# A hybrid attention and recurrence layer on one core: 24 more Strassen pairs in place of 48 classical projection blocks, with the recurrence before the attention

## The chip, the core and the metric

The kernel runs on one core of one Trainium2 chip. The metric is the device time of one execution in microseconds (us). Five engines work side by side, each with its own instruction stream taken in order: TensorE (PE in the profile; its weight loads are PEld), VectorE (DVE), ScalarE (ACT), GpSimd (POOL) and SyncE (SP). They meet at semaphores. Transfers are issued from the streams of SP, ACT and POOL.

## The reference

One layer on 528 tokens (16 learned meta tokens and 512 of x; the reference pads to 640 and drops the padding and the meta tokens at the end), width 2048:

```python
h = rms_norm(x, norm_g)
proj = h @ w_in                       # 2048 x 12368
(q_a, k_a, v_a, z_a, q_i, k_i, w_i, q_b, f_b, i_b, z_b, gates) = jnp.split(proj, cuts, axis=-1)
...
o_a = dsa_attention(q, k, v, qi, ki, wi, chunk_ids, topk)   # 8 heads, top 128 keys of an indexer
y_a = o_a.reshape(B, T, BRANCH_WIDTH) * jax.nn.silu(z_a)
...
o_b = hgrn2_chunkwise(qb, 1.0 - f, vb, jnp.log(f))          # 8 heads of a gated recurrence
y_b = rms_norm(o_b, hgrn_out_norm_g).reshape(...) * jax.nn.silu(z_b)
p = jnp.einsum('btnc,ncd->btnd', y, w_branch)               # two products, 1024 x 2048 each
g = jax.nn.sigmoid(gates)
return x + jnp.sum(g * p, axis=2) @ w_out                   # 2048 x 2048
```

All is float32. Keys, values, forget gates (f_b) and recurrence inputs (i_b) are needed at the meta tokens too; queries, z and gates are not.

## The kernel before

Tokens lie along the columns. hH and hL hold the normalised input, transposed, as 16 tiles of 128 x 528: a high part, and what the high part leaves of the float32 value. Each weight chunk is split in the same way (line 374: ScalarE copies the high part wh, VectorE subtracts for the low part wl), and a product is three matmuls: high by high, high by low, low by high (line 1440).

**Classical blocks.** A job "in" (lines 1413 to 1423) makes 128 columns of the projection out of 16 such tiles of 128 rows: 48 matmuls of 512 columns, or, where the meta tokens are needed, 96 of 264 columns in two PSUM banks. The order is indexer keys, indexer queries, z of attention, keys, values, queries, then by head q, f and i of the recurrence, and z of the recurrence last.

**Strassen pairs.** The gates are made two blocks at a time (run_pair, line 1153). The products of a 2 x 2 split of weights and tokens are done with seven multiplications of half size in place of eight: 7 x 8 x 3 = 168 matmuls of 256 columns, over weight sums s1 to s4 and token sums t1 to t4. The token sums are made once (tops_task, line 1112), the weight sums for each pair: s1 and s2 by VectorE into tiles of their own (lines 401 to 410), s3 and s4 by accumulating DMA from GpSimd's queue (line 112). VectorE combines the products into the two gate blocks, ScalarE applies the sigmoid, SP writes them to DRAM (d_pair, line 1382). The output product uses eight pairs of the same kind (run_out, line 1234).

**What sets the order.** The program is written out by hand with a planner in it. Core (line 43) counts a clock for each engine from fixed costs, while instructions are emitted; attention, recurrence and indexer are generators (tasks) that yield the time at which they can go on, and pump (line 219), called between matmuls of a block, runs a task's next step when its time has passed on the TensorE clock by 300 ns (MARGIN) and VectorE's clock isn't too far ahead. finish (line 231) drives a task to its end with nothing between. Buffers come from 67 slots of 128 x 528 and six PSUM banks of 512 columns and a double one. Weight chunks of 512 KB are loaded from SP's queue into a ring of six, and split two or three products ahead (split_upto, line 364).

Attention runs beside the query blocks, the recurrence beside its own blocks, and a recurrence head waits until all attention heads are through (line 896). Before the first gate pair all tasks are finished (line 1514). y of both branches goes through DRAM (spill_y, line 749); load_y (line 1319) brings it back for the branch products, whose 16 steps load two gate blocks each (req_br, line 1395). After the branch products, m_task (line 1333) makes the token sums for the output.

Of the kernel before, what the change touches and what calls it, by code (L numbers as in the profile page):

```python
# [16 lines left out]
D = 2048  # L17
# [22 lines left out]
MARGIN = 300.0  # L40


class Core:
# [68 lines left out]
    def dma_add(self, out, a):  # L112
        self.nc.gpsimd.dma_start(out, a, accum_op=OP.add)
        return self.at("pool", 4000.0, [out], [out, a])
# [64 lines left out]
def hybrid_kernel(ctx, tc, x, meta, vecs, w_in, rows, w_branch, w_out,  # L179
# [8 lines left out]
    S = Slots(E, sp, [f"s{i}" for i in range(67)], [128, T], None)  # L188
# [42 lines left out]
    def finish(t):  # L231
        while not t.done:
            pump(1e9)
            if t.done:
                break
            nxt = [u for u in tasks if u.t > E.clk["pe"]]
            if nxt:
                E.clk["pe"] = max(E.clk["pe"], min(u.t for u in nxt))
            else:
                assert any(u.step() for u in list(tasks)), "stuck"  # L240
# [8 lines left out]
    def pair(name, keep=0):  # L249
        while len(B2.free) <= keep:  # L250
            yield WAIT
        return B2.get(name)

# [54 lines left out]

    w_in2 = w_in[0]
# [17 lines left out]
    class Pair:  # L327

        def __init__(self, kind, c0, c1, k0, k1, nk, ncols, n=0, done=None, more=()):
            self.kind, self.c0, self.n, self.done, self.nk, self.ncols = kind, c0, n, done, nk, ncols
            self.meta, self.pre, self.req, self.more = False, None, None, more
            self.raw = {}
            for nm, c, k in (("11", c0, k0), ("21", c1, k0), ("22", c1, k1), ("12", c0, k1)):
                ch = self.raw[nm] = {"job": self, "k0": k, "nk": nk, "c0": c, "ncols": ncols, "i": len(stream)}
                stream.append(ch)
            self.ops = []
            for nm in ("11", "s2", "12", "s3", "s1", "22", "s4"):
# [4 lines left out]
    state = {"dma": 0, "split": 0}  # L344
    early = []
    NRAW = 6
    NWS = 3
# [26 lines left out]
    def hi_lo(k, src, m):  # L374
# [3 lines left out]
        (E.ptt if k < 6 else E.tt)(l[:, :m], src, h[:, :m].bitcast(F32), OP.subtract)  # L378
# [22 lines left out]
    def sum_1(pr):  # L401
        if not hasattr(pr, "s1"):
            load_upto(pr.raw["22"]["i"])
            pr.s1 = wp.tile([128, 1024], F32, name=f"sum1_{pr.raw['11']['i']}", tag="s1")
            E.tt(pr.s1, pr.raw["21"]["raw"], pr.raw["22"]["raw"], OP.add)

    def sum_2(pr):
        if not hasattr(pr, "s2"):
            pr.s2 = wp.tile([128, 1024], F32, name=f"sum2_{pr.raw['11']['i']}", tag="s2")
            E.tt(pr.s2, pr.s1, pr.raw["11"]["raw"], OP.add)  # L410

    def sum_3(pr):
        if not hasattr(pr, "s3"):
            pr.s3 = pr.raw["21"]["raw"]
            E.dma_add(pr.s3, pr.raw["11"]["raw"])

    def sum_4(pr):
        if not hasattr(pr, "s4"):
            pr.s4 = pr.raw["12"]["raw"]
            E.dma_add(pr.s4, pr.s2)  # L420

    def prep_op(k, op):

        pr, nm = op["pair"], op["name"]
        first = pr.raw["11"]["i"]
        load_upto(first + (0 if nm == "11" else 2 if nm == "s2" else 3))
        raw = {c: ch["raw"] for c, ch in pr.raw.items() if "raw" in ch}
        if nm in raw:
            src = raw[nm]
        else:  # L430
            for f in (sum_1, sum_2, sum_3, sum_4)[:int(nm[1]) if nm != "s1" else 1]:
                f(pr)
            src = {"s1": pr.s1, "s2": pr.s2, "s3": raw["21"], "s4": raw["12"]}[nm]
        h, l = hi_lo(k, src, 1024)
# [3 lines left out]
        used = {"s3": 2, "22": 3, "s4": 4}.get(nm)  # L438
        if used:
            load_upto(first + used - 1 + NRAW)  # L440

# [154 lines left out]
    def idx_task(j, xq):  # L596
# [18 lines left out]
        if not score:  # L615
            score.extend(slots("score", 4))
# [30 lines left out]
        if not idx_left[0]:  # L647
            S.put(kkH, kkL, CQ, SQ)
            for qt in range(4):
                topk_tasks.append(spawn(topk_task(qt), 6))  # L650

    topk_tasks = []
    bias = [cp.tile([128, k], BF16, name=f"bias{k}") for k in KQ]

    def topk_task(qt):
        kq = KQ[qt]
        sc = score[qt][:, :kq]
        E.dve([sc], [], 64, lambda v: v.memset(sc[0:64, kq - 64:kq], NEG))
        ws = slot("tk")
        w = ws[:, :kq]  # L660
        m8 = cp.tile([128, 8], F32, name=f"m8_{qt}")
        src = sc
        for r in range(TOPK // 8):
            E.dve([m8], [src], kq, lambda v: v.max(m8, src))
            e = E.dve([w], [src, m8], kq, lambda v: v.match_replace(w, m8, src, NEG))
            src = w
            yield e
        E.tt(w, w, sc, OP.is_equal)
        e = E.ts(bias[qt], w, BIAS, None, OP.mult)
        S.put(ws, score[qt])  # L670
        yield e


    kTH, kTL, vH, vL = {}, {}, {}, {}
    vx3 = []
    kx = {}
# [10 lines left out]

    def ka_task(g, xk):
        kx[g] = xk
# [9 lines left out]
        yield e  # L699
        kTH[g], kTL[g] = slot("kTH", F32R), slot("kTL", F32R)  # L700
# [3 lines left out]
        if len(kTH) == 4:  # L704
            pb = yield from bank("pkm")
            for i in range(4):
                e = E.tr(pb[:16, 128 * i:128 * i + 128], kx[i][:, 0:16], ident)
            S.put(*kx.values())
            yield e
            y, e = yield from norm_rope(pb[:16].rearrange("p (b d) -> p b d", b=4), 16, 4,  # L710
                                        tabK[:16, 4:5, :].to_broadcast([16, 4, 64]), "km")
            B1.put(pb)
            yield e
            pb = yield from bank("pkm")
            e = back_T(y, 16, pb)
            yield e
            for i in range(4):
                e = split_T(kTH[i], pb[:, 16 * i:16 * i + 16], 1, kTL[i], 0, 16)
            S.put(y)
            B1.put(pb)  # L720

    def va_task(g, xv):
        pb = yield from bank("pva")
# [3 lines left out]
        vH[g], vL[g] = slot("vH", F32R), slot("vL", F32R)  # L727
        if not vx3:
            vx3.extend((slot("vMH", F32R), slot("vML", F32R), slot("v3")))
        vMH, vML, v3 = vx3  # L730
        E.act(vH[g][:, :512], pb, AF.Copy)
        e = E.tt(vL[g][:, :512], pb, vH[g][:, :512].bitcast(F32), OP.subtract)
        e = E.act(v3[:, 128 * g:128 * g + 128], pb[:, 384:512], AF.Copy)
# [6 lines left out]
        gs = slice(128 * g, 128 * g + 128)  # L740
        E.act(vMH[:16, gs], pm[:16, :128], AF.Copy)
        e = E.tt(vML[:16, gs], pm[:16, :128], vMH[:16, gs].bitcast(F32), OP.subtract)
# [3 lines left out]
    zs = {}  # L746
    yd = [[tc.dram_tile([128, 512], F32, name=f"yd{n}_{h}") for h in range(8)] for n in range(2)]

    def spill_y(n, h, s, e):
        yield e  # L750
        nc.sync.dma_start(yd[n][h], s[:, :512])
        S.put(s)

# [3 lines left out]
    def qa_task(h, xq, prev):  # L757
        g = h // 2
        pb = yield from bank("pqa")
# [9 lines left out]
        yield e  # L769
        qH, qL = slot("qH", F32R), slot("qL", F32R)  # L770
# [4 lines left out]
        while prev and not prev.done:  # L775
            yield WAIT
        for t in topk_tasks + ka_tasks + va_tasks:
            while not t.done:
                yield WAIT
        sm = small[h % 2]  # L780
        ps, pbs, vs = {}, {}, {}
        for qt in (3, 2, 1, 0):
            kq = KQ[qt]
            sl = slice(128 * qt, 128 * qt + 128)
            if kq > 512:
                pb = yield from pair("plg")
                parts = [(pb[:, c, :264], slice(264 * c, 264 * c + 264)) for c in range(2)]
                vs[qt] = pb[:, :, :264]
            else:
                pb = yield from bank("plg")  # L790
                parts = [(pb[:, :kq], slice(0, kq))]
                vs[qt] = pb[:, :kq]
            pbs[qt] = pb
# [4 lines left out]
            if qt == 3:  # L798
                e3 = e
        S.put(qH, qL)  # L800
        yield e3
        col = lambda qt, i: sm[:, 4 * qt + i:4 * qt + i + 1]
        for qt in (3, 2, 1, 0):
            kq = KQ[qt]
            xs = ps[qt] = slot("lg")
            f2 = (lambda a: a.rearrange("p (a b) -> p a b", a=2)) if kq > 512 else (lambda a: a)
            E.dve([xs, sm], [pbs[qt], bias[qt]], kq, lambda vv: vv.tensor_tensor_reduce(
                f2(xs[:, :kq]), vs[qt], f2(bias[qt][:, :]), SC, NEG, OP.add, OP.max, col(qt, 0)))
            (B2 if kq > 512 else B1).put(pbs[qt])
            E.ts(col(qt, 1), col(qt, 0), -1.0, None, OP.mult)  # L810
            e = E.act(xs[:, :kq], xs[:, :kq], AF.Exp, bias=col(qt, 1), accum_out=col(qt, 2))
            if qt == 3:
                e3 = e
        yield e3
        for qt in (3, 2, 1, 0):
            E.dve([sm], [sm], 1, lambda vv: vv.reciprocal(col(qt, 3), col(qt, 2)))
            e = E.ts(ps[qt][:, :KQ[qt]], ps[qt][:, :KQ[qt]], col(qt, 3), None, OP.mult)
        pv_tasks.append(spawn(pv_task(h, ps, e), 1))
# [3 lines left out]
    def pv_task(h, ps, e):  # L822
        g = h // 2
        gs = slice(128 * g, 128 * g + 128)
# [4 lines left out]
        vMH, vML, v3 = vx3  # L829
        po = yield from bank("pov")  # L830

        def turn(b):
# [6 lines left out]
            if b >= 0 and b < 3:  # L839
                S.put(ps[b])  # L840
            if b == 2:
                S.put(ps[3])
# [4 lines left out]
        for b in (3, -1, 0, 1, 2):  # L847
            n = 512 - 128 * max(b, 0)
            kp = 128 if b >= 0 else 16
            if b == 3:  # L850
                tH, tL = slot("pT"), None
                e = E.act(tH[:, :n], pb[:, :n], AF.Copy)
            else:
# [771 lines left out]
```

## Time and profile before

| | |
|---|---|
| median of 3 runs | 1593.71 us (1593.67 to 1596.26) |
| span of the profiled execution | 1593.3 us |
| busy: TensorE, VectorE, ScalarE, GpSimd | 1577.0, 1008.1, 587.4, 112.2 us |
| DMA | 200.94 MB, mean 126 GB/s |
| granted TensorE clock | 0.999 |

Stages by the timeline: start and indexer to about 160 us, z of attention to 241, attention's blocks to 482, recurrence blocks to 830, z of the recurrence to 932, gate pairs to 1250, branch products to 1430, output to the end.

How to read it: a row of a group has line, engine, operation, tile written and tiles read, shapes, count, then busy us in all and mean ns of one, then idle time before and what ended it. A row of a timeline has start, length, engine, line, operation and tiles. A row of windows has the stretch, its length, busy time and count for each engine, granted clock, DMA share and GB/s. A row of transfers has tiles, queue, count, size and median us from issue to landing. Matmuls overlap in the pipeline, so that the lengths of two add up to more than the time between their starts.

### The profile page before, as it was taken

To read this page: it belongs to the slowest core of one execution; us is meant where nothing else is said; L and a number is where in the kernel's file an instruction comes from. 1 tells how busy PE (TensorE), PEld (TensorE's weight loads), DVE (VectorE), ACT (ScalarE), POOL (GpSimd) and SP (SyncE) were. 2 spreads that over 40 slices of the span, in tenths; PEclk is the share of its full clock that TensorE was granted. 3 is DMA by queue.
4 is the path that set the end of the run, shared out by engine and by line. 5 is a ranking of instruction groups with operands and counts; after the bars stand their busy time and mean duration, and the time that the engine had idled before them with its cause. 6 is when DMAs were issued, how large, how long until landed. Compare 5 with 4: busy or idle time off the path is not lost.

```text
span 1593.3 us, 28292 instructions
## 1 busy us (share of the span) xinstructions
PE 1577.0 (99%) x11752; PEld 1427.3 (90%) x11752; DVE 1008.1 (63%) x1773; ACT 587.4 (37%) x910; POOL 112.2 (7%) x108
## 2 busy tenths in 40 slices
PE   7999999999999999999999999999999999999998
PEld 6888889998889888889997899999999888889998
DVE  6687899436666545444444886666666543778765
ACT  5555422324444222222222344444444331334342
POOL 3100000000000000000000000000000000002222
PEclk9999999999999999999999999999999999999999
DMA  9222333232232232222232457777777864448783
GB/s 255 80 68 79 99 93 93 81 91 75 60 79 74 74 81 67 80 68 79 68 81 80 120 128 186 186 186 186 186 187 184 255 198 132 145 120 225 212 215 90
DMA packets 284817, 200.94 MB, mean 126 GB/s; under 512 B 9428, under 2 KB 263904, under 8 KB 284688
## 3 DMA queue, kind: packets, MB, share of 16 engines
q1 hardware_dynamic: 272208, 167.58, 36.9%
q0 software_dynamic: 6976, 25.25, 9.1%
q10 hardware_dynamic: 5504, 6.29, 1.2%
q8 instruction: 92, 1.51, 0.4%
q14 instruction: 37, 0.30, 0.1%
HBM read 157.16 MB, written 16.78 MB: 109 GB/s over the span
## 4 chain that ended last, share of the span: by engine, by line
PE 97%; DVE 1%; DMA 1%; issue 1%; ACT 1%; POOL 0%; DVEq 0%; ACTq 0%; POOLq 0%
PE pg L90 57%; PE po L88 10%; PE py L88 6%; PE px L88 6%; PE pz L88 5%; PE pw L88 3%; PE phl L90 1%; PE pov L88 1%; PE psc L90 1%; PE plg L90 1%; PE pho L90 1%; PE ppt L94 1%; PE phs L90 1%; PE px L94 1%; PE pqa L94 0%
## 5 line engine op out<-in xcount | busy, mean ns | idle before, releaser
L104 DVE TENSOR_TENSOR wl<-raw,wh 128x1024 fp32r<-128x1024 f32 x276 | 339.9, 1232 | 241.3 <-ACT wh L98 237.4
L90 PE MATMUL pg<-hH,wh 128*128 128x264 f32 (+1 forms) x1392 | 478.8, 344 | 0.0
L98 ACT ACTIVATE wh<-raw 128x1024 fp32r<-128x1024 f32 x278 | 294.2, 1058 | 491.4 <-PE pg L90 258.9
L90 PE MATMUL pg<-hH,wl 128*128 128x264 f32 (+1 forms) x1392 | 464.1, 333 | 0.0
L90 PE MATMUL pg<-hL,wh 128*128 128x264 f32 (+1 forms) x1392 | 462.6, 332 | 0.0
L90 PEld LDWEIGHTS pg<-hH,wl 128*128 128x128 f32 x1392 | 261.6, 188 | 26.3
L90 PEld LDWEIGHTS pg<-hL,wh 128*128 128x128 f32 x1392 | 262.3, 188 | 21.1
L90 PEld LDWEIGHTS pg<-hH,wh 128*128 128x128 f32 x1392 | 261.7, 188 | 21.7
L88 PE MATMUL po<-wh,mh 128*128 128x256 f32 x896 | 159.4, 281 | 0.5 <-DVE xq L104 0.5
L88 PEld LDWEIGHTS po<-wh,mh 128*128 128x128 f32 x896 | 137.7, 189 | 0.8 <-DVE xq L104 0.7
L88 PE MATMUL po<-wl,mh 128*128 128x256 f32 x448 | 125.9, 281 | 0.0
L90 PE MATMUL pg<-yH,wh 128*128 128x512 f32 x256 | 101.1, 395 | 0.4 <-ACT yH L98 0.4
L90 PE MATMUL pg<-yL,wh 128*128 128x512 f32 x256 | 100.9, 394 | 0.3 <-DVE yL L104 0.3
L90 PE MATMUL pg<-yH,wl 128*128 128x512 f32 x256 | 100.9, 394 | 0.0
L88 PEld LDWEIGHTS po<-wl,mh 128*128 128x128 f32 x448 | 84.3, 188 | 0.0
L104 DVE TENSOR_TENSOR wl<-sum,wh 128x1024 fp32r<-128x1024 f32 x48 | 64.9, 1352 | 29.7 <-ACT wh L98 29.7
L98 ACT ACTIVATE wh<-sum 128x1024 fp32r<-128x1024 f32 x48 | 50.9, 1061 | 84.0 <-PE pw L88 27.5
L88 PE MATMUL px<-hL,wh 128*128 128x256 f32 x256 | 72.5, 283 | 0.0
L88 PE MATMUL px<-hH,wl 128*128 128x256 f32 x256 | 72.0, 281 | 0.0
L88 PE MATMUL px<-hH,wh 128*128 128x256 f32 x256 | 71.6, 280 | 0.0
L90 PEld LDWEIGHTS pg<-yL,wh 128*128 128x128 f32 x256 | 48.2, 188 | 12.3 <-DVE yL L104 1.1
L90 PEld LDWEIGHTS pg<-yH,wh 128*128 128x128 f32 x256 | 48.0, 187 | 11.9 <-ACT yH L98 0.8
(309 smaller groups left out, 2594.7 us busy)
## 6 DMA issues: line engine op xcount, KB each, us to landing
raw<-in_w_in_dram SPq DMA_DIRECT2D x192, 512.0 KB, 3.9
raw<-in_w_branch_dram SPq DMA_DIRECT2D x32, 512.0 KB, 4.5
raw<-in_w_out_dram SPq DMA_DIRECT2D x32, 512.0 KB, 4.2
raw<-raw POOLq DMA_DIRECT2D x24, 512.0 KB, 5.4
raw<-sum POOLq DMA_DIRECT2D x24, 512.0 KB, 6.3
gd<-gate SPq DMA_DIRECT2D x32, 256.0 KB, 5.9
g<-gd SPq DMA_DIRECT2D x30, 256.0 KB, 3.0
x<-in_x_dram SPq DMA_DIRECT2D x16, 256.0 KB, 5.4
```

Of the source, the lines that this page charges most:

```text
L88: self.nc.tensor.matmul(out, lhsT, rhs, start=start, stop=stop, skip_group_check=True)
L90: self.nc.tensor.matmul(out, lhsT, rhs, start=start, stop=stop)
L94: self.nc.tensor.transpose(out, in_, ident)
L98: self.nc.scalar.activation(out, in_, f, **kw)
L104: self.nc.vector.tensor_tensor(out, a, b, op=op)
```

## The change

Of the classical blocks only the indexer's and z of attention stay. The other 48 are coupled into 24 pairs of the same kind as the gate pairs: f with q and i with z of each recurrence head, keys with two query heads and values with the other two, each time one block that needs the meta tokens with one that doesn't. The 11 and 12 products, which go to the x bank, take the meta columns along (272 columns). The order becomes recurrence pairs, attention pairs, gate pairs; attention's tasks start once the eighth recurrence head is done, group by group. The branch products begin with the recurrence's branch (ORDER), and y of attention is due at their step 4. A block that waits for its task goes to DRAM when fewer than eight slots are free (hold), and is fetched back on ScalarE's queue (held). The weight sums are made in the loaded chunks themselves, in another order of the seven products; of each split, VectorE's half is put off until the third k step of the next product. That frees room for four more slots. Gates are written without sigmoid, which ScalarE does in the branch stage. Token sums are made beside the z blocks. The meta keys' three matmuls with values become one over 96 rows. One task does top-k for the four query blocks in turn, and some steps of the softmax and the recurrence go from VectorE to ScalarE.

```diff
+NZA = 8
+NSLOT = 71
+ORDER = (1, 0)
+LIMIT = 2000.0
+ROOMY = 8
...
+    SEVEN = (("11", "11", "x", 0), ("s3", "t3", "y", 0), ("12", "21", "x", 1), ("s2", "t2", "v", 0),
+             ("s1", "t1", "z", 0), ("22", "t4", "w", 0), ("s4", "22", "z", 1))
...
+    def sum_w(pr, nm):
+
+        if nm in pr.did:
+            return
+        pr.did.add(nm)
+        load_upto(pr.first + {"s3": 1, "s2": 2, "s1": 2, "s4": 3}[nm])
+        r = {c: ch["raw"] for c, ch in pr.raw.items() if "raw" in ch}
+        if nm == "s3":
+            E.dma_add(r["21"], r["11"])
+        elif nm == "s2":
+            E.tt(r["21"], r["21"], r["22"], OP.add)
+        elif nm == "s1":
+            E.tt(r["11"], r["21"], r["11"], OP.subtract)
+        else:
+            E.dma_add(r["12"], r["21"])
...
     def ka_task(g, xk):
-        kx[g] = xk
+        while not (len(pv_tasks) >= 2 * g and pv_tasks[2 * g - 1].done if g else len(hg_tasks) == 8 and hg_tasks[7].done):
+            yield WAIT
+        xk = yield from held("xk", xk)
+        yield from room(2)
...
+    def fetch(name, of, q, n=512):
+        s = slot(name)
+        q.dma_start(s[:, :n], of[:, :n])
+        E.wr[s.tensor.name] = (E.clk["pe"] + 4000.0, "dma")
+        return s
+
+    def hold(s, n=T):
+
+        if len(S.free) >= ROOMY:
+            return s, None, None, n
+        state["held"] += 1
+        d = tc.dram_tile([128, n], F32, name=f"held{state['held']}")
+        return None, d, spawn(spill(d, s, E.wr[s.tensor.name][0], n), 0), n
+
+    def held(name, x):
+        s, d, t, n = x
+        if s is None:
+            while not t.done:
+                yield WAIT
+            yield from room(1)
+            s = fetch(name, d, nc.scalar, n)
+            yield E.wr[s.tensor.name][0]
+        return s
...
+            elif b < 0:
+                E.mm(o, vm[0:96, 0:128], tH[0:96, :n], False, False, loose=True)
                 S.put(tH)
...
             for k in range(8):
-                th, tl = TB[k][tn]
+                th, tl = TB[k][tn + "m" if wide else tn]
                 st_ = k == 0 and not on_
                 E.mm(b, op["h"][k], th, st_, False, loose=True)
                 E.mm(b, op["h"][k], tl, False, False, loose=True)
                 E.mm(b, op["l"][k], th, False, k == 7, loose=True)
+                if k == WHEN:
+                    flush()
+                    if i == 0:
+                        sum_w(pr, "s2")
+                        sum_w(pr, "s1")
+                pump(LIMIT)
...
             if last:
-                if i == 3:
-                    S.put(*hH[:8], *hL[:8])
-                    ysplit = split_y(load_y(0), 0)
-                elif i == 4:
-                    S.put(*[t for k in range(8) for t in TB[k]["tiles"][:2]])
+                if i == 4:
+                    S.put(*hH[:8], *hL[:8], *[t for k in range(8) for t in TB[k]["tiles"][:2]])
+                    finish_y(ORDER[0])
+                    ysplit = split_y(load_y(ORDER[0]), ORDER[0])
...
+            if (n, p) == (ORDER[0], 4):
+                finish_y(ORDER[1])
+                yr = load_y(ORDER[1])
+                splits[ORDER[1]] = spawn(split_y(yr, ORDER[1]), 5)
...
+    order = [za_pair(h) for h in range(NZA, 8, 2)]
     for h in range(8):
...
+        order += hgrn_pairs(h)
+    for g in range(4):
+        order += attn_pairs(g)
+    order += [gate_pair() for _ in list(gates)]
+    for c0, c1, meta, done in order:
+        jobs.append(Pair("pair", c0, c1, 0, 8, 8, 128, done=done, meta=meta))
```

More of the change, by code (lines that the diff above doesn't have):

```diff
@@ L239, in finish @@
             else:
-                assert any(u.step() for u in list(tasks)), "stuck"
+                any(u.step() for u in list(tasks)) or stuck("fin")
     need = [2]
@@ L252, in pair, with room @@
         return B2.get(name)
+    def room(n, first=False):
+        while len(S.free) < n + (0 if first else keep[0]):
+            yield WAIT
+    keep = [0]
     def slots(name, n=1, dt=F32):
@@ L337, in __init__ @@
                 stream.append(ch)
+            self.first = self.raw["11"]["i"]
             self.ops = []
-            for nm in ("11", "s2", "12", "s3", "s1", "22", "s4"):
+            for nm in (x[0] for x in SEVEN):
                 op = {"pair": self, "name": nm, "prep": len(preps_)}
@@ L703, in ka_task @@
         B1.put(pb)
[L704 to L720, printed above, removed]
+        yield from room(2)
+        pb = yield from bank("pkm")
+        e = E.tr(pb[:16, :128], xk[:, 0:16], ident)
+        S.put(xk)
+        yield e
+        y, sq = slots("km", 2)
+        yield from km_norm(pb[:16, :128], y, sq)
+        e = E.tr(pb[:, 128:144], y[:16, :128], ident[:16, :16])
+        S.put(y, sq)
+        yield e
+        yield split_T(kTH[g], pb[:, 128:144], 1, kTL[g], 0, 16)
+        B1.put(pb)
     def va_task(g, xv):
+        while not (len(pv_tasks) >= 2 * g and pv_tasks[2 * g - 1].done if g else len(hg_tasks) == 8 and hg_tasks[7].done):
+            yield WAIT
+        xv = yield from held("xv", xv)
+        yield from room(3)
         pb = yield from bank("pva")
@@ L758, in qa_task @@
         g = h // 2
+        while prev and not prev.done or g not in va_tasks or not (ka_tasks[g].done and va_tasks[g].done):
+            yield WAIT
+        xq = yield from held("xq", xq)
+        yield from room(3)
         pb = yield from bank("pqa")
@@ L774, in qa_task @@
         yield e
-        while prev and not prev.done:
+        while not topk_tasks or g not in va_tasks or not all(
+                t.done for t in (topk_tasks[0], ka_tasks[g], va_tasks[g], *pv_tasks[:h - 1])):
             yield WAIT
-        for t in topk_tasks + ka_tasks + va_tasks:
-            while not t.done:
-                yield WAIT
+        yield from room(3)
         sm = small[h % 2]
-        ps, pbs, vs = {}, {}, {}
+        ls = slots("lg", 3)
+        ps = {3: ls[0], 2: ls[1], 1: ls[2][:, 0:272], 0: ls[2][:, 272:416]}
+        col = lambda qt, i: sm[:, 4 * qt + i:4 * qt + i + 1]
         for qt in (3, 2, 1, 0):
@@ L828, in pv_task @@
         yield e
-        vMH, vML, v3 = vx3
+        vm = vM[g]
         po = yield from bank("pov")
@@ L884, in hybrid_kernel @@
     on_tasks = []
-    AT = [None, None]
+    AT = []
     LB = []
     def lb_task():
-        while not all(t.done for t in qa_tasks):
+        while idx_left[0]:
             yield WAIT
+        yield from room(2)
+        AT.append(slot("attn"))
+        E.pool([AT[0]], [], T // 2, lambda v: v.memset(AT[0], 0.0))
         LB.append((yield from pair("phl")))
@@ L894, in hgrn_task @@
     def hgrn_task(h, prev):
-        q, f, k, vx = (hg[h][i] for i in ("q", "f", "k", "v"))
-        while (prev and not prev.done) or not all(t.done for t in qa_tasks):
+        while not LB or not mask_t[0].done or (prev and not prev.done):
             yield WAIT
-        while not LB:
-            yield WAIT
-        at = AT[h % 2]
-        mt, vt = slot("mt"), slot("vt")
+        f = yield from held("f", hg[h]["f"])
+        q = yield from held("q", hg[h]["q"])
+        vx = yield from held("v", hg[h]["v"])
+        yield from room(3)
+        at = AT[0]
+        k, vt = slots("hk", 2)
+        E.act(k[:, :528], f[:, :528], AF.Copy, scale=-1.0, bias=1.0)
         pm = LB[0][:, 1, :]
@@ L1511, in hybrid_kernel @@
             job.req()
-        if job.kind == "gate":
+        if job.kind == "pair":
             npair += 1
-            if npair == 1:
-                for t in hg_tasks + on_tasks + t_task:
-                    finish(t)
-                while tasks:
-                    finish(tasks[0])
-                late += [lambda: place_t3(0), lambda: place_t3(4)]
-            last = npair == len(pairs)
+            last = npair == npairs
             run_pair(job, None if last else jobs[ji], late, last)
```

579 lines of the change are left out of this document (331 added, 248 removed).

## The prediction

> **What bounds the kernel now.** I read the page first (shares, chain), then the windows by stage, then what TensorE waited for, then single matmuls by time.
>
> ```profile
> span 1593.3 us, 28292 instructions
> PE 1577.0 (99%) x11752; PEld 1427.3 (90%) x11752; DVE 1008.1 (63%) x1773; ACT 587.4 (37%) x910; POOL 112.2 (7%) x108
> PE 97%; DVE 1%; DMA 1%; issue 1%; ACT 1%; POOL 0%; DVEq 0%; ACTq 0%; POOLq 0%
> ```
>
> The chain that ended last is TensorE from end to end. The waits of TensorE (us in total, times, longest) say the same:
>
> ```profile
> PE pc L94 <- DMA vrow<-in_vecs_dram: 8.2, 1, 8.2
> PE pg L90 <- POOL el L108: 0.8, 1, 0.8
> ```
>
> After one wait of 8.2 us at the start nothing costs it a full microsecond. So the time is the sum of matmul spacings, and an edit is worth what it takes out of that sum. Busy time doesn't show spacing, since matmuls overlap; starts do. Four pairs of rows: a plain block (512 columns) over 56 spacings, a block with meta tokens (264 columns) over 44, the first matmul of two gate pairs 14 pairs apart, and the same pair stage as a window (columns: PE, PEld, DVE, ACT, POOL busy; clock; DMA share; GB/s):
>
> ```profile
> 1289.80 0.40 PE L90 MATMUL pg<-yH,wl 128*128 128x512 f32 x1
> ...
> 1302.74 0.39 PE L90 MATMUL pg<-yL,wh 128*128 128x512 f32 x1
> ```
> ```profile
> 241.62 0.28 PE L90 MATMUL pg<-hH,wh 128*128 128x264 f32 x1
> ...
> 246.94 0.28 PE L90 MATMUL pg<-hH,wl 128*128 128x264 f32 x1
> ```
> ```profile
> 951.93 0.28 PE L88 MATMUL px<-hH,wh 128*128 128x256 f32 x1
> ...
> 1230.44 0.28 PE L88 MATMUL px<-hH,wh 128*128 128x256 f32 x1
> ```
> ```profile
> 569.70:613.30 43.60, 43.60 (x467) 39.25 (x466) 21.67 (x45) 10.42 (x18) 1.01 (x1) 1.00 0.28 74
> 951.93:971.82 19.89, 19.89 (x170) 19.89 (x169) 12.78 (x14) 8.80 (x11) 1.70 (x2) 1.00 0.77 186
> ```
>
> 12.94 us / 56 = 231.1 ns for 512 columns; 5.32 / 44 = 120.9 ns for 264; 278.51 / 14 = 19.89 us for a pair of 168 matmuls, so 118.4 ns for 256. In the pair window the weight load (PEld) is busy all the time: halving the columns doesn't quite halve the spacing (115.5 ns would be half).
>
> **The change part by part.** *48 blocks become 24 pairs.* Each couple is one block with meta tokens (96 matmuls of 264 columns) and one without (48 of 512): 96 x 120.9 + 48 x 231.1 = 11.61 + 11.09 = 22.70 us. Its pair has 168 matmuls, 120 of 256 columns and 48 (the x bank, which carries the meta columns) of 272. No row has 272 columns at full width; 8 columns more cost 2.5 ns from 256 to 264, so I estimate 123.4 ns: 120 x 118.4 + 48 x 123.4 = 14.21 + 5.92 = 20.13 us. Saved: 2.57 us a couple, 61.7 us for 24.
>
> Here a rule speaks against the change. The row says 231.1 ns for 512 columns. The Trainium skill, "TensorE: Matmul & The Clock Gate", section "Back-to-back issue gap", gives about 131 ns for 512 columns and 81 ns for 128 in sustained streams with weight loads; a line between them (my estimate) puts 256 near 98 ns, and a couple would be cheaper than its pair by about 0.7 us. By that rule the change would cost some 18 us. The trace disagrees (231.1 ns), and it decides.
>
> *The first 16 meta keys in attention.* Three 16-row matmuls become one of 96 rows and 512 columns, per head:
>
> ```profile
> 375.44 0.50 PE L88 MATMUL pov<-pTH,vMH 16*128 16x512 f32 x1
> 375.78 0.39 PE L88 MATMUL pov<-pTL,vMH 16*128 16x512 f32 x1
> 376.01 0.38 PE L88 MATMUL pov<-pTH,vML 16*128 16x512 f32 x1
> 376.33 0.44 PE L94 MATMUL ppt<-ident,lg 128*128 128x128 f32 x2
> ```
>
> Three cost 0.89 us, one between 0.23 and 0.34; I take 0.3, so 0.59 x 8 heads = 4.7 us. Other task matmuls keep their number and are only moved.
>
> *VectorE.* A pair splits seven weight sums instead of four chunks, forms two sums and combines banks:
>
> ```profile
> L104 DVE TENSOR_TENSOR wl<-raw,wh 128x1024 fp32r<-128x1024 f32 x276 | 339.9, 1232 | 241.3 <-ACT wh L98 237.4 <-DMA yd<-zs 3.6
> 160.00:240.00 80.00, 80.00 (x355) 65.32 (x354) 72.44 (x202) 24.97 (x32) 0.00 (x0) 1.00 0.35 96
> 569.70:613.30 43.60, 24.44 (x81) 15.05 (x80) 7.35 (x6) 0.00 (x0) 1.00 0.28 74
> 282.59 0.43 DVE L118 TENSOR_SCALAR bias<-tk 128x528 bf16<-128x528 f32 x1
> ```
>
> A pair needs 12.78 us of VectorE in 19.89, a couple four splits, 4.93 us: 24 x 7.85 = 188 us more, about 1,195 of 1,550. The densest stretch is the recurrence. One head (window 569.70:613.30, VectorE 21.67, of which 7.35 are splits) by the second window row, that of the splits alone, leaves 14.3 us of its own; what goes to ScalarE (about 1.4) the moved gate and silu of z bring back. Two pairs and a head then make 2 x 12.78 + 14.3 = 39.9 us of VectorE in 2 x 20.13 + (43.60 - 11.09 - 2 x 11.61 = 9.3) = 49.6 us, 80%. In 160:240 it was 91% busy (72.44 of 80) beside top-k and TensorE lost nothing. Matmul weights are prepared two to three products (5.7 to 8.5 us) ahead, so short queues are covered. Top-k ended at 282.59, 41 us after the last z block (241.62); the sums of the tokens now come before it, so I estimate that 45 us of it fall into the first pairs. I take 5 us for all of this; ends: 0 (as in 160:240) and 27 (rival two).
>
> *Waiting blocks go to DRAM and back.* Writes stand on SP's queue with the weight loads, which are a pair and more ahead: nothing. Fetches stand on ScalarE's queue; behind each are weight halves, due two products later: nothing. But a fetched block's first user is often a transpose on TensorE, issued when the program's own clock has counted 4.0 us and a margin of 0.3; its matmul of 256 columns is counted as 109.4 ns where 118.4 pass, so 4.3 becomes 4.65 us.
>
> ```profile
> xq<-in_x_dram ACTq DMA_DIRECT2D x12, 256.0 KB, 4.0
> yr<-yd ACTq DMA_DIRECT2D x8, 256.0 KB, 5.2
> raw<-raw POOLq DMA_DIRECT2D x24, 512.0 KB, 5.4
> ```
>
> Such fetches landed in 4.0 and 5.2 us. 24 of them (8 v, 4 + 4 + 8 of attention) go to TensorE directly. With 5.2, the row from DRAM scratch, (5.2 - 4.65) x 24 = 13 us; ends 0 (4.0) and about 48 (2 us each, if ScalarE reaches the issue late). By the Trainium skill, "DMA: Bandwidth & Descriptors", section "Anatomy of one DMA", 2.0 us and bytes at 436 GB/s (its fit is for GpSimd's queue), 2.6 us would do: by that page the term is nothing and the sum 13 us lower; both rows here are longer.
>
> *Sums in place, two of them by accumulating DMA.* Both are issued three products (8.5 us) before their split and take 5.4 (row above): hidden. POOL holds them in order, with the tasks' powers behind: up to 4 us later for a task, none for TensorE.
>
> *Start of the branch products.* The y tiles are now fetched after product 5 of the last pair, not 4, 2.84 us later:
>
> ```profile
> 1241.90 4.66 ACTq L1322 DMA_DIRECT2D yr<-yd  x8
> 1247.62 1.66 ACT L98 ACTIVATE yH<-yr 128x512 fp32r<-128x512 f32 x3
> ...
> 1250.33 0.40 PE L90 MATMUL pg<-yH,wh 128*128 128x512 f32 x1
> ```
>
> Now the first is in two parts about as the branch matmuls begin (1247.62 plus two operations against 1250.33). Nothing is left of that cover, so +2.8 us. Sigmoids of the gates move to ScalarE in the branch stage, one step ahead: hidden.
>
> *Output.* One more GpSimd addition stands between product 4 and the subtractions after product 5; VectorE waits some 2 us in four places with weights prepared ahead: 2 us, ends 0 and 5.
>
> Sum over the span: 1593.3 - 61.7 - 4.7 + 13 + 5 + 2.8 + 2 = 1549.7. The median (1593.71) stands 0.4 above this execution's span: **1550 us**.
>
> **The rivals.** *One, slower: the serial chain of heads misses its due point.* Recurrence heads follow one another, then attention by groups of two heads, each group only after the last one's values; everything must be over before branch step 4, where the program drains it with no other matmuls to run. Lengths of a head's steps now: recurrence 569.73 to 604.51 and one operation; keys 253.97 to 263.25 and their meta part 299.75 to 307.75; queries to weights 353.46 to 367.87; values 372.08 to 382.95:
>
> ```profile
> 569.73 0.60 PE L94 MATMUL phv<-ident,hv 128*128 128x128 f32 x4
> 604.51 0.69 DVE L104 TENSOR_TENSOR on<-pho,hsq 128x512 f32<-128x512 f32 x1 [1.21 <-POOL hsq L108]
> ```
> ```profile
> 253.97 0.38 PE L94 MATMUL pka<-ident,xk 128*128 128x128 f32 x2
> 263.25 0.74 DVE L125 SCALAR_TENSOR_TENSOR kTL<-pka,gq,kTH 128x512 fp32r<-128x512 f32 x1
> 299.75 0.60 PE L94 MATMUL pkm<-ident,xk 128*16 128x128 f32 x4
> 307.75 0.23 DVE L125 SCALAR_TENSOR_TENSOR kTL<-pkm,gq,kTH 128x16 fp32r<-128x16 f32 x1 [0.51 <-ACT kTH L98]
> 353.46 0.44 PE L94 MATMUL pqa<-ident,xqa 128*128 128x128 f32 x2
> 367.87 0.29 DVE L118 TENSOR_SCALAR lg<-lg,small 128x144 f32<-128x144 f32 x1
> 372.08 0.27 PE L94 MATMUL ppt<-ident,lg 128*128 128x128 f32 x1
> 382.95 0.68 DVE L104 TENSOR_TENSOR zs<-pov,zs 128x512 f32<-128x512 f32 x1
> ```
>
> A recurrence head: 35.5 us and three fetches in a row of 5.2, 51 us (its two pairs bring data every 49.6). A group: 5.2 + 10.0 + 8.2 + 2 x (5.2 + 14.7) + 11.6 = 75 us. From the second pair's end (241.6 + 40) the chain ends at 282 + 8 x 51 + 4 x 75 = 990. Due: 241.6 + 24 x 20.13 + 16 x 19.89 + 8 x 9.3 + eight branch blocks of 5.55 = 1162, without attention's own matmuls. 172 us spare; slot shortage, with two to eight free buffers, can stretch the chain. Beyond 172 each microsecond is lost. To be slower than before it must stretch by some 216 us, 31%: 1594 and more. Chance 0.06.
>
> *Two: VectorE becomes the bound while top-k, sums and recurrence overlap.* In the first 130 us of pairs it has 6.5 x 12.78 + 2 x 14.3 + 45 = 157 us of work; if the order made TensorE wait for all of it, 27 us more, and with late fetches (2 us each) 1550 + 22 + 35 = 1607 at most, 1575 in the middle. Against it: the 91% row, and that tasks step back when VectorE's count runs ahead. Chance 0.15.
>
> *Three: pairs save nothing,* since foreign matmuls between narrow ones hurt where the weight load is already full (19.89 of 19.89), 1593.3 - 4.7 + 23 = 1612. The gate pairs show no tasks beside them, so this is open, but output pairs run beside other tasks. Chance 0.02. The rule of the Trainium skill above, with its 18 us, would give 1630 and has less than 0.01 of that, since the trace's 231.1 ns contradicts it.
>
> **How the numbers follow.** Forecast (1530 to 1565) 0.77; rival two 0.15; rival one 0.06; three 0.02. Low end: no waits anywhere, 1593.3 - 66.4 + 0.4 = 1527. High end: rival two with most of the late fetches, 1588; beyond it lie 0.08 of the two slower cases and a little of rival two. The runs before spread over 2.6 us, 0.16%, so 0.2% is about what can be told from no change. Faster 0.92 (forecast and rival two), same 0.01, slower 0.07.
>
> **What would show it.** Right: pair periods of 20.1 us where no task runs, a recurrence head every 49 to 52 us, attention over before the last gate pair, TensorE's waits on transposes of fetched blocks a dozen microseconds together, VectorE near 80% in the recurrence. Wrong: a period of 20.5 or more without tasks, TensorE waiting on wl, or an idle stretch at branch step 4.

## The result, and the profile after

| | before | after |
|---|---|---|
| median | 1594.99 us (1593.67 to 1596.77) | 1545.26 us (1543.59 to 1546.90) |
| span of the profiled execution | 1593.3 us | 1543.7 us |
| busy: VectorE, ScalarE, GpSimd | 1008.1, 587.4, 112.2 us | 1156.2, 689.4, 160.7 us |

The ratio is 0.969 (0.9676 to 0.9703): faster by 3.1%, 4.7 us below the 1550 forecast. Line numbers of the helpers shift by five to seven (matrix products L93 and L95, transposes L99, ScalarE L103, two-operand VectorE L109). The page of the changed kernel:

```profile
span 1543.7 us, 30244 instructions
PE 1514.8 (98%) x12312; PEld 1425.1 (92%) x12312; DVE 1156.2 (75%) x1954; ACT 689.4 (45%) x1049; POOL 160.7 (10%) x170
PE 35%; DMA 2%; DVE 1%; ACT 1%; issue 0%; ACTq 0%; DVEq 0%
```

TensorE still bounds the kernel. The chain's shares sum to 39% only, so the trail was lost on the way, and the waits have to carry the reading. TensorE's waits of the changed kernel (us in total, times, longest):

```profile
PE pc L99 <- DMA vrow<-in_vecs_dram: 7.7, 1, 7.7
PE px L93 <- ACT p L103: 2.7, 2, 1.3
PE pov L93 <- ACT pT L103: 2.4, 4, 0.7
PE pz L93 <- DVE r L109: 2.3, 3, 0.9
PE pka L99 <- DMA xk<-held: 2.3, 1, 2.3
PE phl L95 <- DVE QA L109: 2.2, 2, 1.1
PE pqa L99 <- DMA xq<-held: 1.2, 1, 1.2
PE pg L95 <- ACT yH L103: 1.2, 1, 1.2
PE pg L95 <- DVE yL L109: 1.2, 1, 1.2
```

Beside the wait at the start, which was there before (8.2 us), three kinds appear that the change could bring: blocks fetched back (3.5 us), VectorE (pz and phl, 4.5 us) and ScalarE with its y tiles (the rest). Starts of the first matmul of two pairs, two pairs apart and with no task between, in the timeline:

```profile
239.19 0.28 PE L93 MATMUL px<-hH,wh 128*128 128x272 f32 x1
...
279.54 0.29 PE L93 MATMUL px<-hH,wh 128*128 128x272 f32 x1
```

40.35 / 2 = 20.17 us a pair, against the 20.13 worked out. VectorE in windows of 80 us (columns as before: PE, PEld, DVE, ACT, POOL), first beside top-k and then in the recurrence:

```profile
240.00:320.00 80.00, 80.00 (x805) 79.17 (x805) 75.80 (x136) 36.20 (x45) 7.43 (x9) 1.00 0.73 166
560.00:640.00 80.00, 80.00 (x872) 77.90 (x871) 60.46 (x98) 33.02 (x46) 7.33 (x8) 1.00 0.70 170
```

95% beside top-k with TensorE busy throughout; 76% in the recurrence.

What differs most from the forecast is the chain of heads. Starts of two recurrence heads and two attention groups, and the end of attention:

```profile
532.05 0.60 PE L99 MATMUL phv<-ident,v 128*128 128x128 f32 x4
579.89 0.60 PE L99 MATMUL phv<-ident,r 128*128 128x128 f32 x4
...
722.56 0.60 PE L99 MATMUL pka<-ident,xk 128*128 128x128 f32 x4
839.12 0.60 PE L99 MATMUL pka<-ident,xk 128*128 128x128 f32 x4
...
1174.75 0.69 DVE L109 TENSOR_TENSOR zs<-pov,zs 128x512 f32<-128x512 f32 x1 [1.09 <-PE pov L93]
```

From the third on, recurrence heads start 46.8 to 53.3 us apart, 49.8 on average, as forecast; the first two, beside top-k, take 75.3 and 65.3, and the recurrence ends at 717 in place of 282 + 8 x 51 = 690. The first attention group takes 116.6 us in place of 75 (the next two 119.6 and 111.7), and the end comes at 1175 in place of 990. (A group is one head of keys and values and two query heads: the keys are coupled with one of the two, the values with the other.) The first matmul of the branch products starts at 1199.10 (a row of it stands further down); eight blocks of 5.55 us put step 4 at 1243.5, and in the trace it starts at 1246.8, behind a slow stretch (last section). So some 70 us were spare, not 172.

### The profile page after: what moved, and what is told of

It is laid out like the page before. It is cut to its first block, busy times and chain, and to the rows that moved or that the text cites. A ratio compares the mean times of both kernels' runs of the same rounds, so it can differ in the third digit from the quotient of the medians.

```text
span 1543.7 us, 30244 instructions
## 1 busy us (share of the span) xinstructions
PE 1514.8 (98%) x12312; PEld 1425.1 (92%) x12312; DVE 1156.2 (75%) x1954; ACT 689.4 (45%) x1049; POOL 160.7 (10%) x170
## 5 line engine op out<-in xcount | busy, mean ns | idle before, releaser
L103 ACT ACTIVATE wh<-raw 128x1024 fp32r<-128x1024 f32 x398 | 421.5, 1060 | 591.9 <-PE pz L93 137.4
L109 DVE TENSOR_TENSOR wl<-raw,wh 128x1024 fp32r<-128x1024 f32 x396 | 485.1, 1226 | 130.8 <-ACT wh L103 124.7
L93 PE MATMUL px<-hH,wh 128*128 128x272 f32 (+1 forms) x640 | 186.9, 292 | 2.7 <-ACT p L103 2.7
L93 PE MATMUL px<-hL,wh 128*128 128x272 f32 (+1 forms) x640 | 182.9, 286 | 0.0
L93 PE MATMUL px<-hH,wl 128*128 128x272 f32 (+1 forms) x640 | 182.8, 286 | 0.0
L93 PE MATMUL po<-wh,mh 128*128 128x256 f32 x896 | 159.3, 281 | 0.5 <-DVE xq L109 0.5
L93 PEld LDWEIGHTS po<-wh,mh 128*128 128x128 f32 x896 | 137.6, 189 | 0.8 <-DVE xq L109 0.7
L93 PE MATMUL po<-wl,mh 128*128 128x256 f32 x448 | 125.8, 281 | 0.0
L93 PEld LDWEIGHTS px<-hH,wh 128*128 128x128 f32 x640 | 120.8, 189 | 3.7 <-ACT p L103 3.1
L93 PE MATMUL pv<-tT,wh 128*128 128x256 f32 x640 | 121.0, 287 | 0.0
L93 PEld LDWEIGHTS px<-hL,wh 128*128 128x128 f32 x640 | 120.8, 189 | 0.0
L93 PEld LDWEIGHTS px<-hH,wl 128*128 128x128 f32 x640 | 120.6, 188 | 0.0
L93 PE MATMUL pz<-tT,wh 128*128 128x256 f32 x640 | 119.4, 286 | 0.0
L109 DVE TENSOR_TENSOR raw<-raw,raw 128x1024 f32<-128x1024 f32 x96 | 117.3, 1221 | 1.6
L93 PE MATMUL pw<-tT,wh 128*128 128x256 f32 x640 | 118.1, 284 | 0.0
L95 PE MATMUL pg<-yH,wh 128*128 128x512 f32 x256 | 101.7, 397 | 1.2 <-ACT yH L103 1.2
L95 PE MATMUL pg<-yL,wh 128*128 128x512 f32 x256 | 101.4, 396 | 1.2 <-DVE yL L109 1.2
L95 PE MATMUL pg<-yH,wl 128*128 128x512 f32 x256 | 101.6, 397 | 0.0
L93 PEld LDWEIGHTS pz<-tT,wh 128*128 128x128 f32 x640 | 99.1, 190 | 0.3
L93 PEld LDWEIGHTS pv<-tT,wh 128*128 128x128 f32 x640 | 98.1, 189 | 0.2
L93 PEld LDWEIGHTS pw<-tT,wh 128*128 128x128 f32 x640 | 97.9, 188 | 0.3
```

The costliest lines, as they stand in the source:

```text
L93: self.nc.tensor.matmul(out, lhsT, rhs, start=start, stop=stop, skip_group_check=True)
L95: self.nc.tensor.matmul(out, lhsT, rhs, start=start, stop=stop)
L103: self.nc.scalar.activation(out, in_, f, **kw)
L109: self.nc.vector.tensor_tensor(out, a, b, op=op)
```

## The experiments

All ratios stand against the kernel before, run on the same chip. Differences in us to the changed kernel are taken across chips; the kernel before took 1593.85 to 1595.02 us beside these runs, so they are good to about 1 us. All edits are to the changed kernel. The last multiplication of a zs tile marks the end of attention ("chain's end").

**What the pairs save.** First, the 16 recurrence couples go back to 32 classical blocks, in the new order, and every block that waits goes through DRAM.

```diff
+            jobs += [Job("in", c0, 128, True, done=copied(f0, d0, True)), Job("in", c1, 128, done=copied(f1, d1, False))]
-        if len(S.free) >= ROOMY:
+        if len(S.free) >= 1000:
```

> The 16 pairs of the recurrence are made as 32 classical blocks again, in the changed kernel's order, with every waiting block still sent through DRAM (all of them, where the changed kernel keeps some in slots); token sums are made beside the sixth head. Theory (the gain is the matmul spacing): 16 x 2.57 = 41 us slower than the changed kernel, 1586 us, 1578 to 1592. Rival (the new order, the freed buffers or the moved work bring the gain): 1545 to 1555 us.

Measured: 1578.96 us, 0.9904 (0.9889 to 0.9919): 33.7 us over the changed kernel, 2.1 us a couple where 2.57 was counted. The classical kernel also waits less: added over all matmuls, starts stand 45.6 us further apart than the median of their shape and output tile, against 50.5 after. That is 4.9 of the missing 7.4 us (6.6 if matmuls are grouped by shape alone). Pairs save what their spacing says, less some waits; that their VectorE work brings these is likely but was not tested. Rival three falls.

Then two more pairs, out of four of the z blocks that were left classical:

```diff
-NZA = 8
+NZA = 4
```

> Four of the eight classical blocks of z become two more pairs, without meta tokens. Theory (each couple saves its matmul spacing, 2 x 11.09 - 19.89 = 2.29 us): 4.6 us less, 1539 to 1543 us. Rival (the token sums, needed 45 us earlier, and top-k with VectorE dense at that point make TensorE wait): 1545 to 1560 us.

Measured: 1547.88 us, 0.9703 (0.9688 to 0.9718): nothing gained. By spacing 2 x (22.18 - 19.89) = 4.6 us go; the same sum of excess spacing rises from 50.5 to 56.8 us. Its waits show where: 8.1 us of them lie between 160 and 400 us, beside the token sums and top-k (0.6 in the changed kernel), and 6.6 of these are on VectorE:

```profile
PE pz L93 <- DVE r L109: 4.6, 5, 2.4
PE pv L93 <- DVE wl L109: 1.5, 2, 1.0
PE py L93 <- DVE wl L109: 0.9, 1, 0.9
```

VectorE had no room for these two pairs.

**What the fetched blocks cost.** The program's clock counts 4.0 us for a fetch; three runs change only that count.

```diff
-        E.wr[s.tensor.name] = (E.clk["pe"] + 4000.0, "dma")
+        E.wr[s.tensor.name] = (E.clk["pe"] + 2000.0, "dma")      # 6000.0, 9000.0
```

> The program's clock counts 2.0 us for a fetched block in place of 4.0, so the first user is issued 2 us earlier. Theory (fetches land in 4 to 5 us, and TensorE stands still for the rest, in order): some 2 us for each of 24 fetched blocks that TensorE reads first, less what other waits of the same task hide: 1560 to 1590 us. Rival (a fetched block's user is held up by other things anyway, so that the count is idle): within 8 us of the changed kernel's 1545.

Measured with 2.0: 1585.29 us, 0.9941 (0.9926 to 0.9956), 40 us slower than after. TensorE's waits on fetched blocks add up to 23.9 us (3.5 in the changed kernel); the longest:

```profile
PE phl L99 <- DMA v<-held: 8.4, 3, 4.0
PE pqa L99 <- DMA xq<-held: 7.9, 3, 3.1
PE pka L99 <- DMA xk<-held: 5.1, 3, 4.1
```

The mechanism that the forecast priced is real: with too small a count, TensorE stands before transposes of blocks that haven't landed. In the changed kernel as it is, the count is nearly right.

> The same count is 6.0 us. Theory (in the changed kernel's trace attention ends at 1175 us and is due at about 1243, 68 us spare): TensorE's 3.5 us of waits on fetched blocks go, the serial chain grows by 2 us for each of some 36 fetches in a row, 72 us at most, which uses up the spare time but no more than that: 1540 to 1552 us. Rival (the chain already decides): up to 70 us slower, 1590 to 1615 us.

Measured with 6.0: 1552.05 us, 0.9733 (0.9719 to 0.9748), 7 us slower, just over the upper edge. The fetch waits are gone from the list, but the chain ends 44 us later, at 1219, so that attention's last steps fall into the last pair and the first 25 us of the branch products, where other waits appear:

```profile
PE pov L93 <- ACT pT L103: 6.3, 4, 4.8
PE pg L95 <- ACT yH L103: 5.7, 1, 5.7
```

> The same count is 9.0 us. Theory (68 us spare, beyond that each microsecond is lost): the chain grows by 5 us for each of some 36 fetches in a row, up to 180 us, so 50 to 112 us beyond the due point, of which TensorE still does attention's own matmuls: 1590 to 1650 us, and an idle stretch of TensorE at branch step 4. Rival (the spare time is the 172 us of the prediction): 1540 to 1555 us.

Measured with 9.0: 1573.32 us, 0.9874 (0.9856 to 0.9892), 28 us slower: below what the theory gave, well above the rival. Chain's end, and the window at branch step 4 (PE busy 26 of 40 us):

```profile
1275.94 0.69 DVE L109 TENSOR_TENSOR zs<-pov,zs 128x512 f32<-128x512 f32 x1 [0.74 <-PE pov L93]
```
```profile
1240.00:1280.00 40.00, 25.95 (x113) 20.83 (x114) 17.49 (x51) 18.44 (x41) 1.85 (x3) 0.79 0.14 41
```

Rival one happens as described: the last matmul of the eighth branch block starts at 1236.4, the first of the ninth at 1275.7, and between them the program drains attention. Its matmuls stand there 25.8 us further apart in all than the medians of their shapes and tiles: most of the 28 us.

**VectorE, and what stands behind it.** All four weight sums on VectorE:

```diff
-            E.dma_add(r["21"], r["11"])
+            E.tt(r["21"], r["21"], r["11"], OP.add)
-            E.dma_add(r["12"], r["21"])
+            E.tt(r["12"], r["12"], r["21"], OP.add)
```

> The two weight sums that accumulating DMAs make (s3 and s4) are made by VectorE as well: 2 x 1.22 us more of it in each pair, 15.2 of 20.1 us, and about 44.8 of 49.6 us (90%) in the recurrence. Theory (VectorE isn't the bound, its queue is covered by weights prepared ahead; in the trace before it was 91% busy beside top-k without a loss): 1543 to 1560 us. Rival (VectorE decides where top-k, sums and recurrence overlap): its 48 x 2.4 = 117 us more show in good part, 1580 us and more, with TensorE waiting on wl.

Measured: 1579.33 us, 0.9902 (0.9885 to 0.9920), 34 us slower: about the rival's time, but not by its waits on wl. The first two pairs, without tasks, take 20.17 and 20.34 us, and the only waits on wl, 1.5 us, are in the output product. The recurrence ends at 810 (717 after), which fits a program whose tasks step back when VectorE's count runs ahead, and attention ends late with it:

```profile
1279.18 0.69 DVE L109 TENSOR_TENSOR zs<-pov,zs 128x512 f32<-128x512 f32 x1 [0.81 <-PE pov L93]
```

The drain at step 4 (1248.3 to 1279.0) loses 18.9 of the 34 us. Two single waits are next: 7.5 us on a copy by ScalarE (pov on pT) and 7.3 us on a fetched v; both are taken up below.

A loss of that kind comes without any VectorE work, by setting the planner's costs to the lengths in the trace (matmul, ScalarE and VectorE operations; three lines of seven):

```diff
-c = max(108.0, n * 0.4167 + 2.7)
+c = max(108.0, n * 0.44 + 5.8)
...
-return self.at("dve", 65 + 1.042 * self.n(out), [out], [a, b])
+return self.at("dve", 152 + 1.05 * self.n(out), [out], [a, b])
```

> The costs that the program's own clock counts are set to the lengths in the trace (a matmul of 256 columns 118 ns for 109, VectorE on 1024 elements 1227 for 1132 and on 256 421 for 332, ScalarE on 1024 1061 for 913). Theory (of the changed kernel's small waits of TensorE, some 16 us after the start, most come from steps issued before their inputs are ready, because the count runs short): 5 to 10 us of them go, 1535 to 1541 us. Rival (they come from landings of DMAs and from ScalarE's order, which this doesn't touch, or the chain gets too long): 1543 to 1560 us.

Measured: 1573.07 us, 0.9853 (0.9834 to 0.9872), 28 us slower: above both expectations, with the rival's long chain as one part. A truer count of VectorE is a fuller one; the recurrence ends at 818, attention at 1276, and the drain (1257.6 to 1275.3) loses 10.6 us. About as much comes from one wait and the slow matmuls behind it:

```profile
PE phl L99 <- DMA v<-held: 9.9, 2, 9.7
```

So truer counts made this kernel slower. Seven lines changed at once, and which of them does it was not tried. To separate the due point from the rest, the VectorE sums again with y of attention due two branch steps later:

```diff
-            if (n, p) == (ORDER[0], 4):
+            if (n, p) == (ORDER[0], 6):
```

> All four weight sums on VectorE as in the run that took 1579 us, and y of attention due at branch step 6 instead of 4, 22 us later. Theory (what that run lost is the serial chain: with VectorE fuller the tasks step back, attention ended at 1279 us where the changed kernel's ended at 1175, and TensorE drained it alone): 15 to 25 us come back, 1553 to 1566 us. Rival (VectorE itself holds TensorE up): 1576 to 1582 us.

Measured: 1568.96 us, 0.9838 (0.9824 to 0.9853): 10.4 us of the 34 come back, less than expected. Attention passes the new due point too (drain from 1279.6 to 1292.8, 8.1 us lost). A timeline of ScalarE at the last pair shows a second cost:

```profile
1176.21 9.88 ACTq L1464 DMA_DIRECT2D yr<-yd  x8
1186.14 0.28 ACT L103 ACTIVATE pT<-ppt 128x128 f32<-128x128 f32 x1 [8.88 <-DMA yr<-yd]
```

The eight issues of y's fetch hold ScalarE's queue for 9.9 us; attention, still running because it is late, has its evictions behind them, and TensorE waits (pov on pT, 8.3 us in one). Most of the 9.9 us is one stand: the seventh issue is over at 1179.9, the eighth begins at 1185.77. It waits for a semaphore that a weight load shares, issued by SP at 1177.55 and landed at 1185.75. With y fetched after product 3 and on SP's queue:

```diff
-                if i == 4:
-                    S.put(*hH[:8], *hL[:8], *[t for k in range(8) for t in TB[k]["tiles"][:2]])
+                if i == 2:
+                    S.put(*hH[:8], *hL[:8])
...
-        (nc.sync if n == ORDER[1] else nc.scalar).dma_start(yr[h][:, :512], yd[n][h])
+        nc.sync.dma_start(yr[h][:, :512], yd[n][h])
```

> All four weight sums on VectorE, y's pairs due from branch step 6 and y fetched on SP's queue after product 3 of the last pair. Theory: what was left of the loss with the sums on VectorE and the due point at step 6 is mostly the eight issues of y's fetch on ScalarE's queue, behind which attention's last pT evictions stood for 8.9 us; with the fetch on SP's queue the wait of the pv product on pT falls from 8.3 us to under 2, and the time is 1552 to 1560 us. Rival: VectorE itself is what costs, in many short waits, and the fetch's place is worth no more than in the kernel with sums on both engines (3.5 us): 1564 to 1570 us.

Measured: 1559.20 us, 0.9782 (0.9765 to 0.9798): 9.8 us less, as the theory had it. What is left is 14 us over the changed kernel. Beside the wait at the start, its three largest waits are not on VectorE:

```profile
PE phl L99 <- DMA v<-held: 7.0, 1, 7.0
PE pov L93 <- ACT pTH L103: 5.1, 1, 5.1
PE ppt L99 <- ACT lg L103: 4.1, 3, 3.1
```

The third lies mostly in a drain again: attention passes step 6 as well (1267.1 to 1281.2, 8.7 us lost). And VectorE stands behind the first. The fetch of v waits for its block's write; the write was issued late on SP's queue, behind a weight load that had waited 14.6 us for VectorE to split an earlier chunk (queues of SP and ScalarE, and SP's waits from 270 to 300 us):

```profile
291.08 1.13 SPq L792 DMA_DIRECT2D held<-r  x2
297.94 0.36 ACTq L797 DMA_DIRECT2D v<-held  x1
SPq L375 <- DVE wl L109: 32.4, 4, 14.6
```

So the 34 us are no direct waits of TensorE on VectorE, of which the run with the sums alone has 6.0 us and the changed kernel 6.5. They are a late chain that is drained at its due point, ScalarE's queue held by y's fetch, and a late write; VectorE's longer work acts through the first and the last.

**The postponed half of the splits.** VectorE's half is issued right behind ScalarE's, as before the change:

```diff
-        if lazy:
+        if False:
```

> VectorE's half of a weight split is issued right after ScalarE's half at the end of a product, not at the third k step of the next (the rest of the change stays). Theory (weights are prepared two to three products ahead, so the order costs TensorE nothing directly, but VectorE, taking its stream in order, stands still for ScalarE's half in front of the combinations and task steps): each product's wait of about 1 us delays tasks, the chain grows by 20 to 60 us and runs into the last pair: 1547 to 1565 us. Rival (putting it off is idle): 1543 to 1547 us.

Measured: 1570.72 us, 0.9850 (0.9834 to 0.9867), 25 us slower than after and above the expectation, though the chain ends earlier (1160). TensorE waits on VectorE directly, and the group of the splits shows why:

```profile
PE phl L95 <- DVE QA L109: 11.4, 15, 2.2
PE pz L93 <- DVE r L109: 9.5, 8, 2.9
```
```profile
L109 DVE TENSOR_TENSOR wl<-raw,wh 128x1024 fp32r<-128x1024 f32 x396 | 486.3, 1229 | 254.8 <-ACT wh L103 246.5 <-DMA raw<-in_w_in_dram 3.4 <-PE plg L95 1.5
```

VectorE stands idle 246.5 us waiting for ScalarE's halves, at the head of its queue, with evictions and task steps behind; in the changed kernel it is 124.7. This part of the change was described but not priced; it is worth 25 us.

**The start of the branch products.** First y fetched after product 3, still on ScalarE's queue (the first diff lines above, without the last pair of lines):

> The y tiles of the first branch are fetched after the third product of the last pair, not the fifth (5.7 us earlier), their buffers being free by then. Theory (the first branch matmuls wait for these tiles): the two waits on yH and yL, 2.4 us, go: 1541 to 1544 us. Rival (the fetch on ScalarE's queue gets in the way of the weight halves behind it, or attention's end does): 1545 us or more.

Measured: 1547.39 us, 0.9703 (0.9688 to 0.9719): no gain. The waits on yH and yL go, and a wait for a bank comes (pz on r, 6.5 us in one); ScalarE's timeline tells why:

```profile
1189.85 7.74 ACTq L1466 DMA_DIRECT2D yr<-yd  x5
1197.71 2.00 ACT L103 ACTIVATE wh<-raw 128x1024 fp32r<-128x1024 f32 x2 [7.96 <-DMA yr<-yd]
```

Five issues hold the queue for 7.7 us and two weight halves stand behind; VectorE's halves wait 6.6 us for them, and the subtraction that frees the bank stands behind those. Then the same on SP's queue (all the lines above, without the change of the due point):

> The y tiles of the first branch are fetched after the third product of the last pair, as in the run that took 1547 us, but on SP's queue. Theory (there the issues stood on ScalarE's queue in front of weight halves, and TensorE waited 6.5 us for a bank): the wait for the bank and the 2.4 us on yH and yL go: 1540 to 1544 us. Rival (the tiles land late on any queue, or the weight loads behind them do): 1545 us or more.

Measured: 1541.72 us (1541.37 to 1542.89), 0.9670 (0.9655 to 0.9684): 3.5 us better than the changed kernel (the times of the two don't overlap, the intervals of their ratios do by a little) and 5.7 us better than with ScalarE's queue at the same place. The eight issues held SP's queue for 5.1 us, and no computing instruction stands on it:

```profile
1186.56 5.06 SPq L1466 DMA_DIRECT2D yr<-yd  x8
```

## Why the prediction was right, and where its terms were not

Adding up, over all matmuls, how far starts stand beyond the median of their shape and output tile gives 32.6 us before and 50.5 after. So of -49.6 us in the span, +17.9 is waits and slow stretches (forecast +22.8), -0.5 the wait at the start, and the rest, -67.0, is spacing (forecast -66.4: 61.7 for the couples, 4.7 for the meta keys, which were not run apart). Grouped by shape alone the sums are 36.4 and 56.9 us, so this split is good to some 3 us. The classical run supports the couples; the meta keys rest on that sum alone. That the waits come out near their forecast is partly luck: one term was more than twice too large, and 5 us that were not foreseen stand against it.

*Fetched blocks, 13 us: mis-sized.* Waits of 3.5 us, and 1.8 in slower matmuls behind one of them (last section). The row of 5.2 us was taken for all, and each user for as early as the count allows; transfers in 245 to 1180 us of the changed kernel (count, KB, median us to landing):

```profile
v<-held ACTq DMA_DIRECT2D x5, 264.0 KB, 2.7
xk<-held ACTq DMA_DIRECT2D x4, 264.0 KB, 4.3
xv<-held ACTq DMA_DIRECT2D x4, 264.0 KB, 5.0
xq<-held ACTq DMA_DIRECT2D x8, 256.0 KB, 4.8
```

By these medians v lands well under the 4.65 us that the program leaves it, attention's blocks at about as much. Of the 24 blocks three v stayed in slots; the other 21 landed 2.6 to 8.3 us after their issue, and their first transposes started 4.7 to 10.6 us after it, 5.7 in the median. The steps run later than the count allows, and only two waits are left.

*VectorE, 5 us:* 4.5 us of waits. Its total is 1156 against 1195 reckoned, its share of the recurrence 76% against 80%. Rival two didn't come: 95% busy beside top-k brought no wait of TensorE between 239 and 325 us, and even the added sums brought only 1.5 us on wl.

*Start of the branch products, 2.8 us:* 2.4 us of waits against 0.7 before, and 1.7 in slow matmuls: 3.4. *Output, 2 us:* 0.5 us on xq, as before. Not foreseen: 5.1 us in ScalarE's late copies (px on p, pov on pT).

*The step that failed without harm is the length of the chain in rival one.* "A group: ... 75 us" took a head's 14.7 us from rows where the logits of four query blocks came back to back, and counted the values of only one head of two, as if the other's ran beside the next queries. In the changed kernel, one head of the first group:

```profile
745.71 0.60 PE L99 MATMUL pqa<-ident,xq 128*128 128x128 f32 x4
...
760.56 0.70 DVE L871 CUSTOM_DVE_ANT_0 lg<-plg,bias 128x528 f32<-128x528 f32 x1
...
767.79 0.30 DVE L871 CUSTOM_DVE_ANT_0 lg<-plg,bias 128x144 f32<-128x144 f32 x1
...
774.96 0.81 ACT L103 ACTIVATE lg<-lg,small 128x272 f32<-128x272 f32 x2
...
787.31 0.69 DVE L109 TENSOR_TENSOR zs<-pov,zs 128x512 f32<-128x512 f32 x1
```

The four logits now pass one after another (starts 760.56 to 767.79; 363.62 to 365.66 in the timeline of the kernel before), the weights are scaled by ScalarE behind its other work, and the next head's queries start only at 785.24, when this head's values are nearly done: the first group's two heads take 42 and 49 us one after the other (in the last two groups heads overlap by some 16 us). Rival one's chance of 0.06 came from a spare of 172 us; with 70 it should have been larger. Three runs (fetch count 9.0, VectorE sums, trace costs) went past the due point, and the drain cost 25.8, 18.9 and 10.6 of the 28 to 34 us that they lost. None became slower than the kernel before. The prediction's "nothing" for the writes held in the changed kernel; with a fuller VectorE a write came too late, as shown above.

*What stays open.* Which of the truer costs makes the order worse, and what the four slots, the meta keys and the steps moved to ScalarE are worth alone, was not tried.

## What to carry to other kernels

When work is moved to a bound engine's shadow, price the serial chain of the moved tasks with their new neighbours, not with lengths from the old order, and say how much is spare at the point where something drains them. Put a burst of DMA issues on a queue that computes nothing: with the same eight issues at the same place the kernel took 1547.4 us from ScalarE's queue and 1541.7 from SP's. A planner's counts steer the order of the program, and making them truer can make it slower.

## What the runs showed of the hardware

A wait of TensorE costs more than its length once it is long enough. After the two waits at the branch's start in the changed kernel:

```profile
1199.10 0.50 PE L95 MATMUL pg<-yH,wh 128*128 128x512 f32 x1 [1.19 <-ACT yH L103]
1200.77 0.59 PE L95 MATMUL pg<-yL,wh 128*128 128x512 f32 x1 [1.18 <-DVE yL L109]
1201.16 0.63 PE L95 MATMUL pg<-yH,wl 128*128 128x512 f32 x1
...
1203.72 0.63 PE L95 MATMUL pg<-yH,wl 128*128 128x512 f32 x1
```

Six spacings from 1201.16 to 1203.72 are 427 ns each in place of 231.1, and the granted clock of 1200 to 1205 us is 0.66, which is what 3.4 us at half the clock would give. It fits that removing 2.4 us of waits brought 3.5: with y fetched on SP's queue the clock of these 5 us is 1.00. Over the fourteen traces of this case, counting a gap as the time between two starts beyond the median of the shape and output tile, every gap of 2.05 us and more (40 of them after the first 60 us) was followed by matmuls at 1.8 to 2 times their spacing, mostly for some 3.4 us, which costs about 1.6 us more, and at times for longer; single gaps up to 1.93 us had no such stretch behind them, and pairs of about 1.4 us in a row had it in some kernels (here) and not in others (the classical run). The Trainium skill, "TensorE: Matmul & The Clock Gate", section "Part 1: The HAM clock gate", has the clock halve after at least one idle window of about 3.4 us and return after about 3.4 us of sustained work: the slow spacing and its length agree, but here gaps of 2.05 us were enough.

Eight issues of 256-KB fetches held the issuing queue for 3.9 to 5.1 us on SP and 4.7 to 9.9 us on ScalarE, where computing instructions behind them waited. One issue took 0.3 to 1.6 us; the long cases are stands in front of an issue whose semaphore an earlier transfer still used. With y fetched early on ScalarE's queue, two of the eight begin at 1192.15 and 1195.60, as weight loads land (1192.13 and 1195.58).
